# Recurrent stages of a two-layer hybrid block: where the high halves are cast, and one scan in place of two

## The chip, the cores and the metric

The kernel runs on one core of a Trainium2 chip. The metric is device time in microseconds (us) of one execution. A core has five engines with instruction queues of their own: TensorE (PE, matrix products, with its weight loads as PEld), VectorE (DVE), ScalarE (ACT), GpSimd (POOL) and SyncE (SP), which issues most of the transfers. Each engine works through its own queue in order; semaphores hold an instruction until what it needs is there.

## The reference, cut to what matters

Two layers are computed over 256 latent tokens and 256 context tokens of 1024 features. Each layer has a mixer (a gated linear recurrence beside a windowed attention, merged by learned gates) and a feed-forward part, both modulated by a condition. The part that concerns us is the recurrence: a centred convolution of width 4 over time, two gates from block-diagonal products (8 blocks of 128 channels), for each of two directions, and a linear scan. The forward scan runs through the context first and hands its last state to the latents; the backward scan does the same in reverse order.

```python
def _lru_coeffs(x, wa, ba, wx, bx, lam):
    r = jax.nn.sigmoid(_block_diag(x, wa, ba)).astype(jnp.float32)
    i = jax.nn.sigmoid(_block_diag(x, wx, bx))
    log_a = LRU_C * r * jax.nn.log_sigmoid(lam.astype(jnp.float32))
    a = jnp.exp(log_a)
    b = jnp.sqrt(-jnp.expm1(2.0 * log_a)) * (i * x).astype(jnp.float32)
    return a, b

def _rglru_branch(x_lat, x_ctx, conv_w, conv_b, wa, ba, wx, bx, lam, need_ctx):
    xl = _dwconv_centred(x_lat, conv_w, conv_b)
    xc = _dwconv_centred(x_ctx, conv_w, conv_b)
    ...
    hc_f = _linear_scan(ac_f, bc_f, None, False)
    hc_b = _linear_scan(ac_b, bc_b, None, True)
    ...
    hl = (_linear_scan(al_f, bl_f, hc_f[:, -1], False)
          + _linear_scan(al_b, bl_b, hc_b[:, 0], True))
    y_lat = hl.astype(x_lat.dtype)
    y_ctx = (hc_f + hc_b).astype(x_ctx.dtype) if need_ctx else None
    return y_lat, y_ctx
```

The second layer needs no output for the context, but its context recurrence still runs, since its last state starts the latents.

## The kernel before, in words

Activations lie with features on the 128 partitions and the 512 tokens along the free dimension, the 256 latents first and the 256 context tokens behind them. Every product of float32 values is made of three products: an operand is split into a high half, rounded to the type fp32r, and a low half, the rest. `mm3` (line 215 of the profile, through `mm`) issues high by high, high by low and low by high into one PSUM bank.

Weights arrive from memory in units of up to 1 MB (pool `wl`, 3 buffers). `split_half` turns 1024 columns of a unit into a high tile `wh` and a low tile `wlo` (4 buffers each): `hi_copy` makes the high half, on ScalarE (line 199) or on VectorE (line 201) by the next letter of `hi_pat`, and `lo_sub` makes the low half on VectorE (line 204). A new `wh` waits until TensorE has used the `wh` of four halves earlier.

The recurrent branch handles its 8 channel blocks in 4 groups of two. For a group, TensorE makes two projections `px` (48 products of 512 columns), two projections `pg` for the output gate (256 columns in the second layer), in the second layer one or more gated attention pieces, and then the gate products of two blocks (`gates`, 24 products, into the 4 PSUM buffers `pa`). Around them:

- `conv` takes `px` through ScalarE (line 876) and three VectorE steps (line 879) into `xf`, and splits it into a pair `xp` (casts of line 201, subtractions of line 204);
- `gates` drains each gate product with a sigmoid on ScalarE (line 893);
- `decays` makes tanh and exp on ScalarE (lines 902, 903) and multiplies the input gate with `xf` on GpSimd (line 904); a square root follows (line 937);
- `recur` makes, for each direction, two products (lines 910, 911) and the scan on VectorE: for the forward direction a scan of the context half (line 913) and one of the latent half that starts from its last column (line 915), for the backward direction one scan over all 512 columns in reverse (line 918). Sum, output gate and split follow (lines 921, 922, 201, and 204 on GpSimd).

The decays of a group are issued with the products of the next one, so that TensorE can go on. TensorE and SyncE keep the order in which the program is written. VectorE, ScalarE and GpSimd get theirs from a scheduler that weighs when inputs should be there; so the order on these engines can change around an edit. The stages in question run at about 252 to 400 us (first layer) and 980 to 1145 us (second layer).

Of the kernel before, what the change touches and what calls it, by code (L numbers as in the profile page):

```python
# [12 lines left out]
ALU = mybir.AluOpType  # L13
# [3 lines left out]
P = 128  # L17
D = 1024
KD = 8
S = 256  # L20
T = 512
L = 2
# [29 lines left out]

# Steps of the early products after the scores, the values and the turned probabilities
# of the last three iterations of the attention, per layer.
FILL = ((2, 0, 0, 2, 2, 0, 2, 0, 0), (2, 1, 0, 2, 1, 1, 1, 0, 0))

# Order of the first phase. A letter is a step, the number its piece:
# f, x, w: load modulation feature tile, token tile, weight unit
# M, C, A, B: modulation products, their row, the row turned to columns, scale and shift
# R, r, N: mean square, rstd, normalised token tile; T: transposed (feature tile, sample)  # L60
# h, H, L: modulated features, float32, high part, low part; K, V: key and value products
# u, U / s, S: high and low half of a weight unit / of a modulation tile
START = """
# [6 lines left out]
"""  # L70
START_F32 = (0, 1)  # modulation feature tiles multiplied as float32, without a split

# [67 lines left out]
def tile_hybrid_block(ctx: ExitStack, tc: tile.TileContext, xin, wstream, mod_start, mod_stream, c_rows,  # L140
# [54 lines left out]

# [1 line left out]
    def hi_copy(eng, dst, src):  # L197
# [23 lines left out]

# [1 line left out]
    dma_units = iter(UNITS)  # L223
# [73 lines left out]

# [1 line left out]
    vt = cst.tile([P, NVEC], F32, name="vt")  # L299
# [14 lines left out]

# [1 line left out]
    def mean_sq(src):  # L316
# [25 lines left out]

# [1 line left out]
    sc_ = cst.tile([P, 16], F32, name="silu_c")  # L344
# [15 lines left out]

# [1 line left out]
    mod_raw = {}  # L362
# [165 lines left out]

# [1 line left out]
    V.tensor_scalar(out=sk[:, 1, :], in0=sk[:, 0, :], scalar1=-1.0, scalar2=None, op0=ALU.mult)  # L530
# [6 lines left out]

# [1 line left out]
    lam = vt[:, VEC["lam", 0]:VEC["lam", 0] + 32]  # L539
# [26 lines left out]

# [1 line left out]
    gg = {}  # L568
# [22 lines left out]
    def mod_columns(l, ch, nv):  # L591
        """Shift or scale of a sublayer: a tile holds the weights of 128 features, one per partition."""
        which, is_sc = divmod(ch, 3)
        if not is_sc:
            for s in range(nv):
                c_bc[s] = tt([P, D])
                nc.sync.dma_start(out=c_bc[s], in_=c_rows[s].partition_broadcast(P))
                A.activation(out=c_bc[s], in_=c_bc[s], func=AF.Silu)  # L598
        cols = [sm.tile([P, KD], F32, tag="mcol", name=nm("mcol"), bufs=4) for _ in range(nv)]
        for ft in range(KD):  # L600
            raw = mod_next()
            for s in range(nv):
                junk = ut([P, D], BF16)
                V.scalar_tensor_tensor(out=junk, in0=raw, scalar=1.0, in1=c_bc[s], op0=ALU.mult, op1=ALU.mult,  # L604
                                       accum_out=cols[s][:, ft:ft + 1])
            if ft < KD - 1:
                yield
        for s in range(nv):
            dst = ab_of((l, which))[:, s, 1 - is_sc, :]
            V.tensor_tensor(out=dst, in0=cols[s], in1=vcol(("bmod", l), ch * 8, 8), op=ALU.add)  # L610
            if is_sc:
                V.scalar_tensor_tensor(out=dst, in0=dst, scalar=1.0, in1=vcol(("gfp" if which else "gmp", l), 0, 8),
                                       op0=ALU.add, op1=ALU.mult)
        if is_sc:
            c_bc.clear()
        yield
# [71 lines left out]
    for l in range(L):  # L688
# [4 lines left out]

# [1 line left out]
        def rope(ps, dst, ctx_too):  # L695
# [18 lines left out]

# [1 line left out]
        def scores(hd, q):  # L716
# [69 lines left out]

        # Products that don't wait for the attention fill its last iterations.
        pre_u, pre_p = [], []
# [51 lines left out]

# [1 line left out]
        tb = []  # L842
# [23 lines left out]

# [1 line left out]
        lead[0] = 100 * l  # L868
        yg = [None] * KD

        def conv(n, ps):
# [9 lines left out]
            xp = pair()  # L881
            split_sb(xf, xp[:, 0, :], xp[:, 1, :])
            return xf, xp

        def gates(n, i, u, xp):
            ri = []
            for dr in range(2):
                rt = tt([P, 2, T])
                for m, bk in ((0, "ba"), (1, "bx")):
                    ps = auxb()  # L890
                    wo = (i * 4 + dr * 2 + m) * P
                    mm3(ps, u.hi(wo, P), u.lo(wo, P), xp[:, 0, :], xp[:, 1, :], True, True)
                    A.activation(out=rt[:, m, :], in_=ps, func=AF.Sigmoid, bias=vcol((bk, l), dr * 8 + n))  # L893
                ri.append(rt)
            return ri

        def decays(n, ri, xf):
            ust = tt([P, 2, T])
            for dr in range(2):
                rt = ri[dr]  # L900
                li = l * 16 + dr * 8 + n
                A.activation(out=ust[:, dr, :], in_=rt[:, 0, :], func=AF.Tanh, scale=hsp[:, li:li + 1])
                A.activation(out=rt[:, 0, :], in_=rt[:, 0, :], func=AF.Exp, scale=nsp[:, li:li + 1])
                G.tensor_tensor(out=rt[:, 1, :], in0=rt[:, 1, :], in1=xf, op=ALU.mult)  # L904
            return ust

        def recur(n, ri, ust, gel):
            for dr in range(2):
                b, a, hs = ust[:, dr, :], ri[dr][:, 0, :], ri[dr][:, 1, :]
                V.scalar_tensor_tensor(out=b, in0=a, scalar=1.0, in1=b, op0=ALU.add, op1=ALU.mult)  # L910
                V.tensor_tensor(out=b, in0=b, in1=hs, op=ALU.mult)  # L911
                if dr == 0:
                    V.tensor_tensor_scan(out=hs[:, S:T], data0=a[:, S:T], data1=b[:, S:T], initial=0.0,  # L913
                                         op0=ALU.mult, op1=ALU.add)
                    V.tensor_tensor_scan(out=hs[:, 0:S], data0=a[:, 0:S], data1=b[:, 0:S],
                                         initial=hs[:, T - 1:T], op0=ALU.mult, op1=ALU.add)
                else:
                    V.tensor_tensor_scan(out=hs[:, ::-1], data0=a[:, ::-1], data1=b[:, ::-1], initial=0.0,  # L918
                                         op0=ALU.mult, op1=ALU.add)
            y = ri[0][:, 1, :N]  # L920
            V.tensor_tensor(out=y, in0=y, in1=ri[1][:, 1, :N], op=ALU.add)
            V.tensor_tensor(out=y, in0=y, in1=gel, op=ALU.mult)
# [3 lines left out]

        hi_pat[0] = "AV"

# [48 lines left out]

# [1 line left out]
        lead[0] = 50 * l  # L979
# [53 lines left out]

# [1 line left out]
        def row_mm(ps, u, kk, srcs, t, first, last):  # L1035
# [32 lines left out]
        class Chain:  # L1068
            """Norm of one token tile of the last product, residual and the next norm, in steps."""

# [211 lines left out]

# [1 line left out]
        def ff_gate(p1, p2):  # L1284
# [176 lines left out]
```

## Time and profile before

| | |
|---|---|
| three runs | 1380.54, 1381.34, 1384.61 us; median 1381.34 us |
| profiled execution, first to last instruction (span) | 1380.7 us; no other time of it is given, and what lies around the span is taken as 0.6 us, the median less the span |
| PE busy | 1329.4 us, 96% of the span |
| DVE busy | 1009.3 us, 73% |
| ACT busy | 649.5 us, 47% |
| POOL busy | 219.4 us, 16% |

The shares are means over the whole program. TensorE is busy nearly everywhere; where it is not, something else sets the pace, and that is read from windows and waits of that stretch. "Busy" of TensorE says that a product was under way, not at which clock; the granted clock stands beside it.

### The profile page before, as it was taken

Reading aid. Unit: us, or ns where it says so; the run is one execution under the profiler, and the core shown is the slowest. Engines: PE = TensorE matmul, PEld = TensorE weight load, DVE = VectorE, ACT = ScalarE, POOL = GpSimd, SP = SyncE. Lnnn points to the kernel's source line nnn. Section 1 sums busy time; section 2 is a strip of 40 time slices with the busy share of each in tenths; the row PEclk is TensorE's granted clock in tenths of the full one; section 3 lists DMA queues with packets and bytes.
Section 4 is the critical chain, followed back from the end, with each engine's and each line's share of the span. In section 5 each row is a group of like instructions: output and inputs, shape, how many; then the busy total and the mean of one; then the engine's idle time right before and its main releaser. Section 6 shows DMA issues by size and latency. Waiting matters only on the chain.

```text
span 1380.7 us, 18865 instructions
## 1 busy us (share of the span) xinstructions
PE 1329.4 (96%) x7372; PEld 1149.0 (83%) x7372; DVE 1009.3 (73%) x1497; ACT 649.5 (47%) x1026; POOL 219.4 (16%) x177
## 2 busy tenths in 40 slices
PE   6999999998989999999999999999999899899998
PEld 3978888876868889888888888899988688899897
DVE  6777687678998765948754754787879998655564
ACT  5766523386642354232212222577487555544342
POOL 1100010024420023101200120310013220102011
PEclk9999999999999999999999999999999999999999
DMA  8510464312257345374555442142333344355552
GB/s 326 211 64 32 138 229 153 106 54 99 92 165 261 123 151 215 107 273 169 191 192 211 162 159 92 62 154 92 108 107 122 122 153 183 123 185 182 193 178 87
DMA packets 37537, 207.98 MB, mean 151 GB/s; under 512 B 4292, under 2 KB 4420, under 8 KB 19784
## 3 DMA queue, kind: packets, MB, share of 16 engines
q1 hardware_dynamic: 37160, 206.24, 42.4%
q8 instruction: 58, 0.95, 0.3%
q10 hardware_dynamic: 288, 0.53, 0.1%
q14 instruction: 31, 0.25, 0.1%
HBM read 205.71 MB, written 1.05 MB: 150 GB/s over the span
## 4 chain that ended last, share of the span: by engine, by line
PE 74%; DVE 16%; issue 5%; ACT 3%; POOL 1%; DMA 0%; DVEq 0%; POOLq 0%; SPq 0%; ACTq 0%
PE pm L215 58%; PE pa L215 14%; DVE wlo L204 3%; DVE t L910 1%; DVE u L879 1%; DVE t L911 1%; DVE u L604 1%; PE pm L765 1%; ACT u L319 1%; DVE wh L201 1%; DVE t L204 1%; DVE t L918 1%; DVE t L913 1%; PE pa L341 1%; DVE t L201 1%
## 5 line engine op out<-in xcount | busy, mean ns | idle before, releaser
L215 PE MATMUL pm<-t,wh 128*128 128x512 f32 (+1 forms) x2672 | 705.4, 353 | 9.7 <-DVE wh L201 2.6
L215 PEld LDWEIGHTS pm<-t,wh 128*128 128x128 f32 x2672 | 473.6, 191 | 78.5 <-DVE wh L201 3.7
L215 PE MATMUL pm<-t,wlo 128*128 128x512 f32 (+1 forms) x1336 | 470.6, 352 | 12.0 <-DVE wlo L204 11.9
L204 DVE TENSOR_TENSOR wlo<-wl,wh 128x1024 fp32r<-128x1024 f32 x265 | 347.2, 1318 | 129.7 <-ACT wh L199 123.8
L199 ACT CAST wh<-wl 128x1024 fp32r<-128x1024 f32 x231 | 240.9, 1051 | 352.0 <-PE pm L215 270.1
L215 PEld LDWEIGHTS pm<-t,wlo 128*128 128x128 f32 x1336 | 255.5, 191 | 46.9 <-DVE wlo L204 14.0
L215 PE MATMUL pm<-wh,t 128*128 128x512 f32 (+1 forms) x784 | 229.0, 372 | 0.0
L215 PEld LDWEIGHTS pm<-wh,t 128*128 128x128 f32 x784 | 143.8, 188 | 25.5
L215 PE MATMUL pa<-t,wh 128*128 128x256 f32 (+1 forms) x768 | 157.2, 304 | 5.1 <-ACT t L893 2.8
L204 POOL TENSOR_TENSOR t<-u,t 128x256 fp32r<-128x256 f32 (+1 forms) x72 | 89.1, 1238 | 452.5 <-DVE t L201 334.5
L215 PE MATMUL pm<-wlo,t 128*128 128x512 f32 (+1 forms) x392 | 145.9, 372 | 0.1
L215 PEld LDWEIGHTS pa<-t,wh 128*128 128x128 f32 x768 | 123.7, 192 | 13.6 <-ACT t L893 8.1
L215 PE MATMUL pa<-t,wlo 128*128 128x256 f32 (+1 forms) x384 | 116.3, 303 | 0.0
L604 DVE SCALAR_TENSOR_TENSOR u<-t,t 128x1024 bf16<-128x1024 f32 x80 | 101.2, 1309 | 1.1 <-ACT t L598 1.1
L215 PEld LDWEIGHTS pm<-wlo,t 128*128 128x128 f32 x392 | 73.8, 188 | 13.2 <-DVE wlo L204 0.5
L215 PE MATMUL pa<-t,t 128*128 128x256 f32 (+1 forms) x480 | 78.0, 311 | 1.1 <-DVE t L204 1.1
L215 PEld LDWEIGHTS pa<-t,wlo 128*128 128x128 f32 x384 | 73.8, 192 | 2.7
L904 POOL TENSOR_TENSOR t<-t,u 128x512 f32<-128x512 f32 x32 | 52.4, 1661 | 101.6 <-ACT t L893 101.4
L215 PEld LDWEIGHTS pa<-t,t 128*128 128x128 f32 x480 | 64.7, 191 | 3.9 <-DVE t L204 1.7
L204 POOL TENSOR_TENSOR t<-t,t 128x512 fp32r<-128x512 f32 (+1 forms) x16 | 29.6, 1852 | 182.7 <-DVE t L201 137.8
L633 DVE SCALAR_TENSOR_TENSOR t<-t,silu_c,t 128x1024 f32<-128x1024 f32 x42 | 56.3, 1361 | 0.4
L329 POOL TENSOR_TENSOR c<-c,negh 128x1 f32<-128x1 f32 x26 | 16.5, 635 | 209.8 <-DVE c L327 193.6
(153 smaller groups left out, 1229.0 us busy)
## 6 DMA issues: line engine op xcount, KB each, us to landing
wl<-in_wstream SPq DMA_DIRECT2D x132, 1024.0 KB, 5.0
t<-in_mod_stream SPq DMA_DIRECT2D x80, 512.0 KB, 4.5
wl<-in_mod_start SPq DMA_DIRECT2D x6, 1024.0 KB, 5.2
wl<-in_wstream SPq DMA_DIRECT2D x12, 512.0 KB, 3.6
t<-in_xin SPq DMA_DIRECT2D x8, 512.0 KB, 4.7
t<-in_c_rows SPq DMA_DIRECT2D x5, 512.0 KB, 6.8
t<-in_mod_start SPq DMA_DIRECT2D x4, 512.0 KB, 8.3
t<-in_g_mix_post SPq DMA_DIRECT2D x3, 512.0 KB, 4.8
```

The source lines that it names most:

```text
L199: A.copy(dst, src)
L201: V.tensor_copy(dst, src)
L204: (G if eng == "G" else V).tensor_tensor(out=dst, in0=src, in1=hi.bitcast(F32), op=ALU.subtract)
L215: PE.matmul(o, lhsT=w, rhs=x, start=bool(start), stop=bool(stop))
L319: A.activation(out=junk[:, :src.shape[-1]], in_=src, func=AF.Square, scale=D ** -0.5, accum_out=ss)
L329: G.tensor_tensor(out=r, in0=ms, in1=negh, op=ALU.pow)
L341: PE.transpose(ps[:, i * P:(i + 1) * P], x[:, ft * P:(ft + 1) * P], ident)
L604: V.scalar_tensor_tensor(out=junk, in0=raw, scalar=1.0, in1=c_bc[s], op0=ALU.mult, op1=ALU.mult, accum_out=cols[s][:, ft:ft + 1])
L633: V.scalar_tensor_tensor(out=accs[s], in0=raw, scalar=cmod[s][:, k:k + 1], in1=accs[s], op0=ALU.mult, op1=ALU.add)
L765: PE.transpose(ps[:, k2, q2 * P:(q2 + 1) * P], probs[q0 + q2][:, (kt0 + k2) * P:(kt0 + k2 + 1) * P], ident)
L879: V.scalar_tensor_tensor(out=o, in0=pv[:, :, max(0, sh):S + min(0, sh)], scalar=cw[kk], in1=o, op0=ALU.mult, op1=ALU.add)
L904: G.tensor_tensor(out=rt[:, 1, :], in0=rt[:, 1, :], in1=xf, op=ALU.mult)
```

## The change

Four edits, all in the recurrent branch:

- `hi_pat` is "A" in place of "AV" during the branch: all high halves of weights there are cast on ScalarE, not every other one on VectorE. After the branch the pattern is as before.
- `conv` casts the high half of `xp` on ScalarE.
- The forward direction holds its values with the context ahead of the latents: its gate products read `xp` with the two halves swapped (a step backwards of 256 columns between the halves), and GpSimd reads `xf` in the same way.
- The forward scan becomes one instruction over 512 columns. The sum of both directions reads the forward result with its halves swapped and is written over the backward result.

The file also lost its comments, and lines behind 882 are numbered a few higher: 893 is now 901, 902 to 904 are 910, 911 and 915, 910 and 911 are 921 and 922, the scans are 925, 921 and 922 are 928 and 929, 937 is 944, 960 is 967.

```diff
             xp = pair()
-            split_sb(xf, xp[:, 0, :], xp[:, 1, :])
+            split_sb(xf, xp[:, 0, :], xp[:, 1, :], hi="A")
             return xf, xp
+
+        def swapped(v):
+
+            return v.rearrange("p (s t) -> p s t", s=2)[:, ::-1, :]
...
-                    mm3(ps, u.hi(wo, P), u.lo(wo, P), xp[:, 0, :], xp[:, 1, :], True, True)
+                    xh, xl = xp[:, 0, :], xp[:, 1, :]
+                    o = ps
+                    if dr == 0:
+                        o, xh, xl = ps.rearrange("p (s t) -> p s t", s=2), swapped(xh), swapped(xl)
+                    mm3(o, u.hi(wo, P), u.lo(wo, P), xh, xl, True, True)
...
-                G.tensor_tensor(out=rt[:, 1, :], in0=rt[:, 1, :], in1=xf, op=ALU.mult)
+                gx = rt[:, 1, :]
+                if dr == 0:
+                    gx = gx.rearrange("p (s t) -> p s t", s=2)
+                G.tensor_tensor(out=gx, in0=gx, in1=swapped(xf) if dr == 0 else xf, op=ALU.mult)
...
-                if dr == 0:
-                    V.tensor_tensor_scan(out=hs[:, S:T], data0=a[:, S:T], data1=b[:, S:T], initial=0.0,
-                                         op0=ALU.mult, op1=ALU.add)
-                    V.tensor_tensor_scan(out=hs[:, 0:S], data0=a[:, 0:S], data1=b[:, 0:S],
-                                         initial=hs[:, T - 1:T], op0=ALU.mult, op1=ALU.add)
-                else:
-                    V.tensor_tensor_scan(out=hs[:, ::-1], data0=a[:, ::-1], data1=b[:, ::-1], initial=0.0,
-                                         op0=ALU.mult, op1=ALU.add)
-            y = ri[0][:, 1, :N]
-            V.tensor_tensor(out=y, in0=y, in1=ri[1][:, 1, :N], op=ALU.add)
+                if dr == 1:
+                    a, b, hs = a[:, ::-1], b[:, ::-1], hs[:, ::-1]
+                V.tensor_tensor_scan(out=hs, data0=a, data1=b, initial=0.0, op0=ALU.mult, op1=ALU.add)
+            y = ri[1][:, 1, :N]
+            y2 = y.rearrange("p (s t) -> p s t", t=S)
+            V.tensor_tensor(out=y2, in0=swapped(ri[0][:, 1, :])[:, :N // S], in1=y2, op=ALU.add)
...
-        hi_pat[0] = "AV"
+        hi_pat[0] = "A"
```

The order on TensorE, SyncE and GpSimd stays the same, instruction for instruction. VectorE and ScalarE are scheduled anew in both recurrent stages. Two places of the first layer show it.

VectorE, at the end of the second group's recurrence, before: `wlo_3096` is the first low half that the third group's projections need; `t_` names are tiles of the recurrence (the scans are listed as SCALAR_TENSOR_TENSOR).

```order
L913 SCALAR_TENSOR_TENSOR t_2843<-t_2843,t_2932 128x256
L910 SCALAR_TENSOR_TENSOR t_2932<-t_2854,t_2932 128x512
L915 SCALAR_TENSOR_TENSOR t_2843<-t_2843,t_2932 128x256
L911 TENSOR_TENSOR t_2932<-t_2932,t_2854 128x512
L201 CAST wh_3095<-wl_2957 128x1024
L918 SCALAR_TENSOR_TENSOR t_2854<-t_2854,t_2932 128x512
L204 TENSOR_TENSOR wlo_3096<-wl_2957,wh_3095 128x1024
```

The same place on VectorE in the changed kernel, where the same low half is called `wlo_3092`:

```order
L925 SCALAR_TENSOR_TENSOR t_2841<-t_2841,t_2930 128x512
L929 TENSOR_TENSOR t_2830<-t_2830,u_2791 128x512
L921 SCALAR_TENSOR_TENSOR t_2930<-t_2852,t_2930 128x512
L201 CAST t_3031<-t_2830 128x512
L922 TENSOR_TENSOR t_2930<-t_2930,t_2852 128x512
L204 TENSOR_TENSOR wlo_3092<-wl_2955,wh_3091 128x1024
L925 SCALAR_TENSOR_TENSOR t_2852<-t_2852,t_2930 128x512
```

The cast of the high half has left VectorE, the two short scans are one, and the low half now stands ahead of the last scan of the group, not behind it.

ScalarE, in the first layer, from the convolution of the group's second block (`u_2779`) to its first sigmoid, before (`u_2791`, `u_2793` are the output gates, which wait for `pg`):

```order
L876 ACTIVATE u_2779<-pm_2670,vt 128x512
L199 CAST wh_2865<-wl_2727 128x1024
L960 ACT_TABLE_LOAD
L960 ACTIVATE u_2791<-pm_2729 128x512
L960 ACTIVATE u_2793<-pm_2754 128x512
L199 CAST wh_2947<-wl_2819 128x1024
L893 ACT_TABLE_LOAD
L893 ACTIVATE t_2821<-pa_2822,vt 128x512
```

The same stretch of ScalarE in the changed kernel:

```order
L876 ACTIVATE u_2779<-pm_2670,vt 128x512
L199 CAST wh_2787<-wl_2643 128x1024
L199 CAST wh_2863<-wl_2727 128x1024
L199 CAST wh_2867<-wl_2727 128x1024
L967 ACT_TABLE_LOAD
L967 ACTIVATE u_2791<-pm_2729 128x512
L199 CAST t_2784<-u_2779 128x512
L199 CAST wh_2945<-wl_2817 128x1024
L967 ACTIVATE u_2793<-pm_2754 128x512
L901 ACT_TABLE_LOAD
L901 ACTIVATE t_2819<-pa_2820,vt 128x512
```

Two more weight casts and the cast of the second block's `xp` (`t_2784`) stand between the convolution and the sigmoids, two of the casts now between the two output gates. No table load is added.

## Rows read from the trace of the kernel before

**Rows 1.** The page's first part: busy us, share of the span, instructions.

```profile
PE 1329.4 (96%) x7372; PEld 1149.0 (83%) x7372; DVE 1009.3 (73%) x1497; ACT 649.5 (47%) x1026; POOL 219.4 (16%) x177
```

**Rows 2.** Windows of both stretches: length, busy us (instructions) by engine, PEclk, DMA.

```profile
290.00:395.00 105.00, 93.57 (x399) 74.99 (x397) 101.35 (x131) 72.08 (x93) 39.09 (x19) 0.97 0.25 84
...
1017.00:1142.00 125.00, 114.44 (x744) 103.14 (x742) 122.70 (x159) 80.29 (x106) 29.52 (x19) 0.97 0.37 127
```

**Rows 3.** Waits of PE, 290:400, then 1000:1160: total us, times, longest.

```profile
PE pm L215 <- DVE wlo L204: 7.8, 2, 6.3
...
PE pm L215 <- DVE wlo L204: 4.1, 4, 1.2
```

**Rows 4.** Timeline of PE: start, us, line, operation, [idle before <-releaser].

```profile
337.34 0.80 PE L215 MATMUL pm<-t,wlo 128*128 128x512 f32 x1 [1.52 <-DVE wlo L204]
...
388.17 0.61 PE L215 MATMUL pm<-t,wh 128*128 128x512 f32 x2
395.05 0.79 PE L215 MATMUL pm<-t,wlo 128*128 128x512 f32 x1 [6.26 <-DVE wlo L204]
```

**Rows 5.** Timeline of DVE: casts and scans, each with what follows.

```profile
330.87 0.68 DVE L913 TENSOR_TENSOR_SCAN t<-t,t 128x256 f32<-128x256 f32 x1
331.47 1.72 DVE L910 SCALAR_TENSOR_TENSOR t<-t,t 128x512 f32<-128x512 f32 x1
333.12 0.74 DVE L915 TENSOR_TENSOR_SCAN t<-t,t 128x256 f32<-128x256 f32 x1
333.78 0.66 DVE L911 TENSOR_TENSOR t<-t,t 128x512 f32<-128x512 f32 x1
334.36 0.68 DVE L201 CAST wh<-wl 128x1024 fp32r<-128x1024 f32 x1
334.96 1.21 DVE L918 TENSOR_TENSOR_SCAN t<-t,t 128x512 f32<-128x512 f32 x1
336.10 1.19 DVE L204 TENSOR_TENSOR wlo<-wl,wh 128x1024 fp32r<-128x1024 f32 x1
...
356.45 0.40 DVE L201 CAST t<-u 128x512 fp32r<-128x512 f32 x1
356.77 0.68 DVE L910 SCALAR_TENSOR_TENSOR t<-t,t 128x512 f32<-128x512 f32 x1
```

**Rows 6.** Groups of DVE by form, 290:395: count, busy us, mean ns, idle before.

```profile
L204 DVE TENSOR_TENSOR wlo<-wl,wh 128x1024 fp32r<-128x1024 f32 x15 | 22.5, 1502 | 0.2
L910 DVE SCALAR_TENSOR_TENSOR t<-t,t 128x512 f32<-128x512 f32 x16 | 16.1, 1014 | 0.0
...
L201 DVE CAST wh<-wl 128x1024 fp32r<-128x1024 f32 x8 | 7.4, 926 | 0.0
...
L201 DVE CAST t<-u 128x512 fp32r<-128x512 f32 x6 | 2.5, 418 | 0.0
```

**Rows 7.** The same by form for 1017:1142.

```profile
L201 DVE CAST wh<-wl 128x1024 fp32r<-128x1024 f32 x13 | 10.5, 809 | 0.0
...
L201 DVE CAST t<-u 128x512 fp32r<-128x512 f32 x6 | 2.5, 420 | 0.1
```

**Rows 8.** Timeline where POOL and DVE run together.

```profile
302.18 5.01 POOL L204 TENSOR_TENSOR t<-t,t 128x512 fp32r<-128x512 f32 x1 [23.10 <-DVE t L201]
311.22 1.61 POOL L204 TENSOR_TENSOR t<-t,t 128x512 fp32r<-128x512 f32 x1 [4.03 <-DVE t L201]
...
306.02 2.25 DVE L204 TENSOR_TENSOR wlo<-wl,wh 128x1024 fp32r<-128x1024 f32 x1
```

**Rows 9.** ACT: casts, 290:395 by form; one whole line's min/median/max.

```profile
L199 ACT CAST wh<-wl 128x1024 fp32r<-128x1024 f32 x10 | 10.1, 1045 | 0.0
...
L1006 ACT ACTIVATE t<-u x16: 401/526/635, 426.3 to 1158.4; 128x512 fp32r<-128x512 f32 x8, 128x256 fp32r<-128x256 f32 x8
```

**Rows 10.** Waits of DVE's weight casts, 240:400, then 970:1180.

```profile
DVE wh L201 <- PE pm L215: 12.3, 2, 9.1
...
DVE wh L201 <- PE pm L215: 4.7, 4, 3.1
```

## The prediction

> **What bounds the kernel now.** I read the page's busy shares first. TensorE is at work for 96% of the span [rows 1], so the kernel as a whole can only gain where TensorE stands still or runs at a lower clock. The windows come next, laid over the two recurrent stages, since the edits touch nothing else. In 290 to 395 us TensorE is busy for 93.57 of 105 us and VectorE for 101.35; in 1017 to 1142 us TensorE for 114.44 of 125 and VectorE for 122.70 [rows 2]. There the reader is to see a change of roles: VectorE has 3.65 and 2.30 us of idle time left, and TensorE 11.43 and 10.56. ScalarE is busy for only 72.08 and 80.29 us. The waits then name the link: of what TensorE waits for, the low halves of weights on VectorE come first, 7.8 us in the first layer and 4.1 in the second [rows 3]. The timeline shows where: 1.52 us at 337.34, and 6.26 us before 395.05, where the products of the next projections have no low half [rows 4]. At 337.34 the instructions just ahead on VectorE are the cast, the backward scan and the subtraction itself, back to back [rows 5]. So in these two stretches the end is set by VectorE's queue, and what is taken out of it moves TensorE forward, as long as TensorE has idle time to give.
>
> The most that both stretches can return: the idle 11.43 + 10.56 = 22.0 us, and the clock. It was granted at 0.97 in both [rows 2]; with levels of 1.2 and 2.4 GHz, 3% of 105 and of 125 us is work lost, at most 3.2 and 3.8 us. Together 29.0 us.
>
> **Weight casts.** VectorE loses 24 casts of 128x1024 over the whole kernel. Eight stood in the first stretch and 13 in the second [rows 6, 7]; by the changed order two and four of them stay on VectorE, since they come when the branch has ended. So 6 and 9 go. The price of one is the distance to the next start, not the duration, because neighbours overlap: 334.96 - 334.36 = 0.60 us [rows 5]. That is 6 x 0.60 = 3.6 and 9 x 0.60 = 5.4 us. The means of 0.93 and 0.81 us [rows 6, 7] are longer, but hold the time that GpSimd costs (below), which the next instruction would meet instead.
>
> **Casts of the convolution.** Of 16, 6 lie in each stretch [rows 6, 7]; one costs 356.77 - 356.45 = 0.32 us [rows 5]. 6 x 0.32 = 1.9 us in each.
>
> **Scans.** A forward direction cost 0.60 us (331.47 - 330.87) and 0.66 (333.78 - 333.12) [rows 5]. A scan over 512 columns has a row of its own, the backward one: 336.10 - 334.96 = 1.14 us [rows 5]. 0.12 us less for each of 8 blocks is 1.0 us in each stretch. The forward one reads upward and not in reverse; I take the same price.
>
> **Order.** At the stall of 337.34 the low half now stands ahead of the group's last scan, not behind it: 1.1 us more there, once, by the same scan. In the second layer I count nothing for order.
>
> **What is added.** ScalarE takes over the casts: 6 x 1.045 us for weights and 6 x 0.635 for the convolution, 10.1 us on top of 72.08 in the first stretch, and 9 x 1.045 + 6 x 0.635 = 13.2 on top of 80.29 in the second [rows 2, 9]. The price for a 512-column cast from SBUF is the longest of line 1006. That gives 82 of 105 and 93.5 of 125 us, or 84% and 80% when each stretch is also shortened as forecast. It fits, so the casts themselves are hidden beside TensorE's products. If that cover were gone, they would cost up to those 23 us. The new waits are what remains: the subtraction for `xp` on VectorE now waits for a cast on another engine, with the next group's scans and low halves queued behind it. Bounds: nothing, if the other work put ahead of it in the new order covers the cast; 16 x 0.635 = 10.2 us if no cast is covered. A cast that comes earlier than on VectorE could even gain a little, but no row shows more than the cast's own 0.32 us, 5 us for 16. I take 1 us lost, near no cost, because in the listed order VectorE has several recurrence steps between the convolution and its subtraction.
>
> **Reversed halves.** 96 gate products (8 blocks, 2 gates, 3 products, 2 layers) and 16 multiplications on GpSimd read two runs of 256 columns in exchanged order. No row shows such a read on these engines. On VectorE the backward scan reads wholly in reverse at the price given. Lower bound: nothing, since the same number of columns is read, and fewer cannot be. Upper bound: every such read takes twice as long. Two products take 0.61 us [rows 4], so 0.3 us more for each, 96 x 0.3 = 29 us; on GpSimd 1.61 us more for each [rows 8], 16 x 1.61 = 26 us, beside other work. I take nothing, as the nearest row, the reversed scan, shows no price.
>
> **GpSimd's share.** In the first stretch the mean low half takes 1502 ns, the mean of line 910 is 1014 ns [rows 6]; undisturbed they take 1.19 and 0.68 us [rows 5]. That is 15 x 0.31 + 16 x 0.33 = 10 us of VectorE's time in two groups alone, spent where GpSimd runs: a GpSimd subtraction of 1.61 us took 5.01 us, and the low half on VectorE at 306.02 took 2.25 [rows 8]. It is tempting to hope that this goes with the casts. The Trainium skill (SBUF — State Buffer, "Who interferes with whom") says that an instruction of VectorE with two SBUF inputs contends with a GpSimd one just as a copy in a fast mode does, and that whichever starts first blocks the other. By that rule the stretching stays, since low halves, products and scans all have two inputs; the rows agree, as it is the low half and line 910 that are stretched. Were it the casts' doing, 10 us more would go. My sum leaves the 10 us where they are.
>
> **Sum.** First stretch 3.6 + 1.9 + 1.0 + 1.1 = 7.6 us, of 11.43 idle; second 5.4 + 1.9 + 1.0 = 8.3, of 10.56 idle. Together 15.9, less 1 for new waits: 14.9. Against the profiled execution: 1380.7 - 14.9 = 1365.8 us of span, and 0.6 around it: 1366.4, say 1366 us. The median shown is 1381.3. What is late next: still the low half after 388 us, with TensorE idle for a few microseconds there, so I count no gain of clock.
>
> **Rivals.**
> - *TensorE never waits in the stretches.* VectorE's queue gets so short that it is always ahead, and the clock stays up: 1381.3 - 29.0 = 1352 us. For it: the idle time of TensorE and what VectorE loses are of one size. Against it: GpSimd's share stays, and the last group's recurrence is a chain that depends on ScalarE's table loads as well. Chance 0.12, all that ends below 1357.
> - *ScalarE's queue eats the gain.* Each cast of the convolution comes late by its own length and the 16 waits cost their upper bound: 1381.3 - 15.9 + 10.2 = 1375.6, and 2 to 5 us more if weight halves come late too: 1378 to 1381. For it: ScalarE works in order, with table loads in between. Against it: a sixth of its time is free. Chance 0.11 for an end within the uncertainty.
> - *Slower: a weight cast blocks the sigmoids.* On VectorE the weight casts waited for TensorE to release a tile, 12.3 us in the first layer (9.1 us the longest) and 4.7 in the second [rows 10]. On ScalarE the output gates and sigmoids stand behind such a wait, and the sigmoids empty the four banks that TensorE fills. It decides from the point where one such wait is longer than TensorE needs to fill four banks, 12 products at 0.3 us or 3.7 us. If the gain is lost but for scans and convolution casts (5.8 us) and the 17 us are TensorE's: 1381.3 - 5.8 + 17.0 = 1392.5 us. Against it: the longest wait, 9.1 us, lay in front of a cast that the new order puts later. Chance 0.06.
> - *The exchanged halves cost at TensorE or GpSimd*: up to 1366 + 29 = 1395 us. The scan in reverse speaks against it. Chance 0.03.
>
> **How the numbers follow.** The likeliest case, VectorE's queue shortened and most of it returned, has 0.68 and reaches from 1357 to 1377 us. About 0.3% (4.1 us) is what a measurement of this kernel can tell from no change. Faster by more than that: 0.68 + 0.12 = 0.80. Within: 0.11. Slower: 0.06 + 0.03 = 0.09. The range for 8 in 10 is 1356 to 1379 us: the likeliest case, the edge of the first rival and the lower half of the second.
>
> **What would show it.** Right: in the changed profile VectorE's casts of weights fall by 24 and those from `u` by 16; the wait of 6.26 us near 395 shrinks by some 4 us or starts 7 to 8 us earlier; the group-to-group distance of the second layer's convolutions shrinks by about 2 us; gate products last as long as before. Wrong: VectorE idle for ScalarE's casts (its waits by `u` and `wh` over 5 us in a stretch), a wait of TensorE for sigmoids that takes the place of those for low halves, or longer gate products.

## The result, and the profile after

The changed kernel took 1366.51 us in the median of 4 runs (1366.32 to 1368.79), the kernel before 1382.7 us on the same chip (4 runs, 1380.54 to 1384.61). The ratio is 0.9887, with a 95% interval of 0.9871 to 0.9903. The prediction said 1366 us, in a range of 1356 to 1379. The profile of the changed kernel is that of its slowest run (1368.79 us, granted clock 0.990; the other three ran at 0.992 to 0.994), so it shows about 2.3 us less of the gain than the median.

The page's first part of the changed kernel, which answers to [rows 1] (span 1367.0 us):

```profile
PE 1323.8 (97%) x7372; PEld 1146.9 (84%) x7372; DVE 983.6 (72%) x1441; ACT 680.8 (50%) x1066; POOL 226.2 (17%) x177
```

VectorE has 56 instructions less (24 weight casts, 16 convolution casts, 16 scans) and ScalarE 40 more. The span is 13.7 us shorter. Of these TensorE's busy time gave 5.6 us (1329.4 to 1323.8) with the same 7372 products, and its idle time 8.1 us (span less busy: 51.3 to 43.2). I had expected nearly all of it from the idle time.

TensorE issues the same products in the same order in both kernels, so a stretch can be laid over exactly the same work. The windows of before, from a gate product of the first layer to the stall at 395.05, and from a gate product of the second layer to the first product behind its last group (length, then busy us and instructions of PE, PEld, DVE, ACT, POOL, then PEclk, DMA share, GB/s):

```profile
329.50:395.05 65.55, 55.09 (x230) 43.83 (x230) 62.17 (x78) 45.82 (x60) 25.83 (x13) 0.95 0.24 82
...
1062.30:1112.50 50.20, 43.75 (x252) 37.92 (x252) 49.85 (x65) 28.82 (x41) 14.07 (x10) 0.93 0.28 95
```

The same work in the changed kernel:

```profile
328.74:387.73 58.99, 52.87 (x232) 42.94 (x231) 55.20 (x64) 48.84 (x64) 27.13 (x13) 0.99 0.24 83
...
1059.10:1100.20 41.10, 39.99 (x253) 35.83 (x253) 40.72 (x50) 34.46 (x48) 19.04 (x10) 1.00 0.31 111
```

In the first pair 6.6 us go: 4.3 us of TensorE's idle time (10.46 to 6.12) and 2.2 of its busy time, at a clock of 0.99 in place of 0.95. In the second pair 9.1 us go: 5.3 us idle (6.45 to 1.11) and 3.8 busy, at 1.00 in place of 0.93. With the same products, the busy time changed almost only where the clock was lower in one of the two kernels, so I count it as clock. The windows of before that lie on the dips show it at the lower of the two levels (1.2 GHz):

```profile
1098.00:1105.00 7.00, 6.28 (x21) 4.94 (x20) 7.00 (x10) 3.81 (x6) 2.01 (x2) 0.52 0.44 152
337.00:340.50 3.50, 3.16 (x8) 2.49 (x9) 3.50 (x7) 3.00 (x5) 0.00 (x0) 0.51 0.20 26
```

Each of these two dips followed upon waits: 1.76 us for a high half at 335.10 and 1.52 for a low half at 337.34 [rows 4], and 1.54 and 0.64 us at 1096.30 and 1097.41. With these waits shortened neither dip is there after. The dip at the last stall of the first layer stayed, and costs more than before: 5.9 us of products ran in it (386.82 to 393.65), before 3.5 us (391.68 to 398.50), as the stall filled the rest. That gives 1.2 us back.

Waits of PE after, 290:400 and then 1000:1160, in the form of [rows 3]:

```profile
PE pm L215 <- DVE wlo L204: 5.4, 1, 5.4
...
PE pa L215 <- ACT t L901: 1.4, 2, 0.7
...
PE pm L215 <- DVE wlo L204: 3.0, 3, 1.2
...
PE pa L215 <- ACT t L901: 1.9, 4, 1.0
```

The 7.8 us of the first layer are 5.4, the 4.1 of the second 3.0; waits for sigmoids are 1.4 and 1.9 (1.8 and 1.0 before). The timeline of PE after, for the products that stand at 337.34 and 395.05 in [rows 4]:

```profile
332.85 0.39 PE L215 MATMUL pm<-t,wlo 128*128 128x512 f32 x1
...
387.73 0.80 PE L215 MATMUL pm<-t,wlo 128*128 128x512 f32 x1 [5.44 <-DVE wlo L204]
```

The wait at 337.34 is gone, and this product starts 4.5 us earlier. The stall of 6.26 us is still one of 5.44, but it begins 6.5 us earlier and ends 7.3 us earlier. The timeline of DVE shows why it still stands there:

```profile
383.72 1.22 DVE L925 TENSOR_TENSOR_SCAN t<-t,t 128x512 f32<-128x512 f32 x1
384.85 1.68 DVE L921 SCALAR_TENSOR_TENSOR t<-t,t 128x512 f32<-128x512 f32 x1
386.46 1.21 DVE L204 TENSOR_TENSOR wlo<-wl,wh 128x1024 fp32r<-128x1024 f32 x1
387.60 0.68 DVE L922 TENSOR_TENSOR t<-t,t 128x512 f32<-128x512 f32 x1
```

VectorE runs without a gap through the last group's recurrence and reaches the low half at 386.46; TensorE starts when it is done. Groups of DVE by form, 290:395, after (as in [rows 6]):

```profile
L204 DVE TENSOR_TENSOR wlo<-wl,wh 128x1024 fp32r<-128x1024 f32 x19 | 28.0, 1476 | 0.1
L925 DVE TENSOR_TENSOR_SCAN t<-t,t 128x512 f32<-128x512 f32 x16 | 19.3, 1209 | 0.0
L921 DVE SCALAR_TENSOR_TENSOR t<-t,t 128x512 f32<-128x512 f32 x14 | 13.1, 942 | 0.3 <-ACT t L944 0.3
```

In the same 105 us VectorE now makes 19 low halves, not 15. Their mean of 1476 ns and the 942 of line 921 (910 before) are nearly as stretched as before: what GpSimd costs (theory D below) has not gone with the casts.

### The profile page after: what moved, and what is told of

Same layout as the page of the kernel before. It is cut to its first block, busy times and chain, and to the rows that moved or that the text cites. A ratio compares the mean times of both kernels' runs of the same rounds, so it can differ in the third digit from the quotient of the medians.

```text
span 1367.0 us, 18844 instructions
## 1 busy us (share of the span) xinstructions
PE 1323.8 (97%) x7372; PEld 1146.9 (84%) x7372; DVE 983.6 (72%) x1441; ACT 680.8 (50%) x1066; POOL 226.2 (17%) x177
## 3 DMA queue, kind: packets, MB, share of 16 engines
HBM read 205.71 MB, written 1.05 MB: 151 GB/s over the span
## 4 chain that ended last, share of the span: by engine, by line
PE 77%; DVE 13%; ACT 4%; issue 4%; POOL 1%; DMA 1%; DVEq 0%; POOLq 0%; ACTq 0%
PE pm L215 61%; PE pa L215 14%; DVE wlo L204 3%; DVE t L925 2%; DVE u L604 1%; PE pm L765 1%; DVE t L921 1%; DVE t L922 1%; DVE t L204 1%; ACT u L319 1%; ACT wh L199 1%; DMA t<-in_xin 1%; DVE u L879 1%; PE pa L341 1%; DVE t L1108 1%
## 5 line engine op out<-in xcount | busy, mean ns | idle before, releaser
L199 ACT CAST wh<-wl 128x1024 fp32r<-128x1024 f32 x255 | 265.7, 1050 | 348.8 <-PE pm L215 270.7
L204 POOL TENSOR_TENSOR t<-t,t 128x512 fp32r<-128x512 f32 (+1 forms) x16 | 35.2, 2197 | 160.7 <-DVE t L201 140.1
```

Of the source, the lines that this page charges most:

```text
L199: A.copy(dst, src)
L204: (G if eng == "G" else V).tensor_tensor(out=dst, in0=src, in1=hi.bitcast(F32), op=ALU.subtract)
```

## The experiments

Theory A is that of the prediction: what leaves VectorE's queue in the two stages comes back on TensorE. Theory B says that it is the new order on VectorE and ScalarE, theory C that the high halves are ready earlier. Theory D says that what is left of the stretching is GpSimd's. Ratios are to the kernel before on the same chip, with their 95% intervals.

**Only the weight casts** (on the kernel before):

```diff
-        hi_pat[0] = "AV"
+        hi_pat[0] = "A"
```

> The kernel before with one edit: all high halves of weights in the recurrent branch are cast on ScalarE. Theory A (VectorE's queue time sets both stretches): 15 casts of 0.60 us leave the stretches, so 9.0 us less than before, 7 to 11. Theory B (the gain comes from the new order on VectorE, low halves ahead of scans): the gain can be anything up to the whole 14 us or near none, and the waits of TensorE change without VectorE's busy time mattering. Theory C (the cast on ScalarE runs beside VectorE, so the low half is ready earlier): the whole gain of the full change is here, 13 us or more.

Measured: 1374.44 us against 1381.8, ratio 0.9946 (0.9933 to 0.996), 7.4 us less. The first layer's stall ends only 1.4 us earlier (393.61), though six casts are gone there, and a new wait stands beside it. (This trace is 0.4 us late already at 249 us, ahead of anything edited.) Waits of PE of this kernel, 290:400:

```profile
PE pm L215 <- DVE wlo L204: 5.3, 1, 5.3
PE pa L215 <- ACT t L893: 4.5, 3, 3.1
```

TensorE waits 4.5 us for sigmoids (1.8 before), 3.14 us of it at 361.53. The timeline of ScalarE shows what these sigmoids, with their table load, stood for:

```profile
355.71 0.60 ACT L960 ACTIVATE u<-pm 128x512 f32<-128x512 f32 x1 [0.45 <-PE pm L215]
359.49 1.28 ACT L893 ACT_TABLE_LOAD   x1 [3.18 <-DVE t L918]
```

ScalarE had its casts behind it and stood idle until VectorE ended a backward scan (line 918, 358.17 to 359.39). So this is VectorE's queue once more, at another place, and not a weight cast that blocks the sigmoids, as the prediction's slower rival has it. In the full change TensorE's wait for sigmoids is 1.4 us.

**Only the convolution's cast** (on the kernel before):

```diff
-            split_sb(xf, xp[:, 0, :], xp[:, 1, :])
+            split_sb(xf, xp[:, 0, :], xp[:, 1, :], hi="A")
```

> The kernel before with one edit: the high half of the convolution's result is cast on ScalarE. Theory A: 12 casts of 0.32 us in the two stretches, 3.8 us less than before, 2 to 5. Theory B: no fixed size. Theory C: no gain or a small loss, since a hop to another engine is added in front of the gate products.

Measured: 1375.2 us, ratio 0.9954 (0.9942 to 0.9967), 6.4 us less. The 3.8 us of the casts lie outside the interval (4.6 to 8.0 us). The stall ends at 391.38, 3.7 us earlier. TensorE's idle time fell by just 3.8 us (span 1373.3 less busy 1325.8 is 47.5, against 51.3) and its busy time by 3.6: what is more than the casts' own time is busy time. Of that, 1.0 us lies ahead of 249 us and 0.6 behind 1151 us, where nothing was edited.

**Only the scan and the exchanged halves** (the changed kernel with both casts put back):

```diff
-        hi_pat[0] = "A"
+        hi_pat[0] = "AV"
...
-            split_sb(xf, xp[:, 0, :], xp[:, 1, :], hi="A")
+            split_sb(xf, xp[:, 0, :], xp[:, 1, :])
```

> The changed kernel with both casts put back as before: context ahead of latents and one forward scan are left. Theory A: 16 times 0.12 us, 2.0 us less than before, 1 to 4 with the order at the stall of the first layer. Exchanged halves read at a price (the rival of the prediction): up to 29 us more than before. Theory C: no change.

Measured: 1380.89 us, ratio 0.9986 (0.9977 to 0.9995), 1.9 us less by the ratio, with an interval of 0.7 to 3.2. With 96 gate products and 16 multiplications reading their halves exchanged, nothing of the 29 us that bounded them appears. The three parts alone sum to 0.54 + 0.46 + 0.14 = 1.14%, the whole change has 1.13%: within the intervals they neither help nor hinder each other.

**VectorE's time put back** (the changed kernel; copies of the casts' shapes into the low tiles, which the subtraction then overwrites; nothing waits for them; 24 of 128x1024 and 16 of 128x512; `rec` is 1 during the branch):

```diff
             hi_copy(hi_pat[0][hi_n[0] % len(hi_pat[0])], hi[:, :n], raw[:, s0:s0 + n])
+            if rec[0] and hi_n[0] % 2 == 1:
+                V.tensor_copy(lo[:, :n], raw[:, s0:s0 + n])
...
+            V.tensor_copy(xp[:, 1, :], xf)
             split_sb(xf, xp[:, 0, :], xp[:, 1, :], hi="A")
```

> The changed kernel, but VectorE makes a copy of the same shape and source for every cast that it lost (24 of 128x1024, 16 of 128x512), into the low half's tile ahead of the subtraction that overwrites it; nobody waits for the copies, and ScalarE makes the high halves as in the changed kernel. Theory A: only the scan is left of the gain, so 1 to 4 us less than before and 11 to 14 us more than the changed kernel. Theories B and C: the high halves still come from ScalarE, most of the gain stays, 10 us or more less than before.

Measured: 1382.04 us, ratio 1.0003 (0.9994 to 1.0012). The whole gain is gone, though ScalarE makes all the high halves and the scan is one. The timeline of PE of this kernel at the stall:

```profile
394.66 0.79 PE L215 MATMUL pm<-t,wlo 128*128 128x512 f32 x1 [5.62 <-DVE wlo L204]
```

It is back at the time of before (395.05). TensorE's busy time is back too, 1329.0 us. VectorE keeps the new order at the end of the second group's recurrence: the low half at 335.98, ahead of the scan at 337.11. So the gain, that of the clock with it, hangs on VectorE's time; B and C fall. Theory A had foretold 1 to 4 us less than before, for the one scan that stays; even that is not seen (0.8 less to 1.7 more by the interval).

**The gate product on VectorE** (the changed kernel):

```diff
-                G.tensor_tensor(out=gx, in0=gx, in1=swapped(xf) if dr == 0 else xf, op=ALU.mult)
+                V.tensor_tensor(out=gx, in0=gx, in1=swapped(xf) if dr == 0 else xf, op=ALU.mult)
```

> The changed kernel with the 32 multiplications of the input gate moved from GpSimd to VectorE. 28 of them lie in the two stretches and add 28 x 0.60 = 16.8 us to VectorE's queue. Theory D (what GpSimd runs beside VectorE is paid in VectorE's time, about 0.55 us for each GpSimd instruction: in 290 to 395 us of the changed kernel low halves, line 921, casts and line 604 are stretched by 11.0 us in all, beside 20 of them): 15.4 us come back, so within 4 us of the changed kernel. Rival (the stretching has another cause than GpSimd): 14 to 17 us more than the changed kernel, and the means of low halves and line 921 stay near 1476 and 942 ns.

Measured: 1361.23 us, ratio 0.9851 (0.9837 to 0.9864), some 5 us less than the changed kernel although VectorE got 32 instructions more. Theory D had foretold a difference of at most 4 us, its rival 14 to 17 us more; the gain goes beyond what D foretold.

**The low half of the result on VectorE** (the changed kernel):

```diff
-            split_sb(y, d[:, 0, :N], d[:, 1, :N], lo="G")
+            split_sb(y, d[:, 0, :N], d[:, 1, :N])
```

> The changed kernel with the 16 subtractions that split the recurrence's result moved from GpSimd to VectorE: 8 x 0.60 + 8 x 0.33 = 7.4 us more in VectorE's queue. Theory D: 16 x 0.55 = 8.8 us come back, so 0 to 3 us less than the changed kernel; the wait of ScalarE for GpSimd (3.75 us at 362 us) goes as well. Rival: 5 to 7 us more than the changed kernel.

Measured: 1370.64 us, ratio 0.9917 (0.9903 to 0.9931), some 4 us more than the changed kernel, where theory D foretold 0 to 3 less and its rival 5 to 7 more: a miss for both. The timeline of DVE of this kernel shows that the stretching goes on:

```profile
334.63 2.23 DVE L204 TENSOR_TENSOR wlo<-wl,wh 128x1024 fp32r<-128x1024 f32 x1
336.79 1.77 DVE L928 TENSOR_TENSOR t<-t,t 128x512 f32<-128x512 f32 x1
338.49 2.30 DVE L204 TENSOR_TENSOR wlo<-wl,wh 128x1024 fp32r<-128x1024 f32 x1
340.71 1.77 DVE L929 TENSOR_TENSOR t<-t,u 128x512 f32<-128x512 f32 x1
```

Low halves take 2.23 and 2.30 us, not 1.21, and lines 928 and 929 take 1.77, not 0.68. GpSimd's gate products, which remain, run beside them, four from 332.10 on for 9.82 us together, and TensorE waits 1.95 us at 336.92 for a stretched low half. Yet the time is not lost here: the stall at the end of this layer is 1.46 us and not 5.44, and behind it the same product starts at 393.06 us, in the changed kernel at 393.01. It is lost in the second layer. The timeline of PE of this kernel, and of the same product in the changed one:

```profile
1102.83 0.76 PE L215 MATMUL pm<-t,wh 128*128 128x256 f32 x2 [3.37 <-DVE wh L201]
```

```profile
1100.18 0.50 PE L215 MATMUL pm<-t,wh 128*128 128x256 f32 x2 [0.76 <-DVE wh L201]
```

At the last gate products the two kernels are level (1087.64 and 1087.60). Then TensorE waits 3.37 us for a high half that VectorE casts behind the last recurrence, and from there to 1109.70 the clock is granted at 0.51 (in the changed kernel at 1.00). In that recurrence lines 921 and 922 and the added subtraction took 1.77, 1.78 and 1.51 us, beside four gate products on GpSimd (8.04 us from 1088.30). That half a move shifted the meeting of both engines fits this, but is argued and not shown.

**No GpSimd in the recurrence** (both edits together):

> Both moves together: nothing of the recurrence runs on GpSimd. VectorE gets 24 us more work in the two stretches. Theory D: about 24 us come back, so within 5 us of the changed kernel, and the means on VectorE are those of undisturbed instructions (1.21 us a low half, 0.68 us line 921). Rival: 18 us or more above the changed kernel.

Measured: 1359.12 us (1358.46 to 1359.75), ratio 0.9833 (0.9819 to 0.9846): the fastest of all, 7.4 us below the changed kernel, where theory D had foretold a difference of at most 5. DVE by form, 290:395, of this kernel:

```profile
L204 DVE TENSOR_TENSOR wlo<-wl,wh 128x1024 fp32r<-128x1024 f32 x19 | 23.2, 1219 | 0.2
...
L921 DVE SCALAR_TENSOR_TENSOR t<-t,t 128x512 f32<-128x512 f32 x14 | 9.5, 687 | 1.0 <-ACT t L944 1.0
L915 DVE TENSOR_TENSOR t<-t,u 128x512 f32<-128x512 f32 x12 | 7.7, 689 | 0.0
```

Both means are at their undisturbed size, 1219 ns for 1476 and 687 for 942. On GpSimd a gate product took 1.71 us in the mean, here 0.69. TensorE's waits in 290:420 are nearly gone:

```profile
PE pa L215 <- ACT t L901: 1.4, 2, 0.7
PE pm L215 <- DVE wlo L204: 1.0, 2, 0.6
```

**More on ScalarE** (the changed kernel; the high half of the result `y` and the six weight casts left on VectorE):

```diff
-            split_sb(y, d[:, 0, :N], d[:, 1, :N], lo="G")
+            split_sb(y, d[:, 0, :N], d[:, 1, :N], hi="A", lo="G")
...
-        hi_pat[0] = "V"
+        hi_pat[0] = "A"
...
-                hi_pat[0] = "V" if j == 4 else "A"
+                hi_pat[0] = "A"
```

> The changed kernel with more of the same: the high half of the recurrence's result and the 6 weight casts that were left on VectorE go to ScalarE too. Theory A: 8 x 0.34 + 8 x 0.20 + 6 x 0.60 = 7.9 us leave VectorE's queue, but TensorE has only 6.8 us of waits left in 290 to 400 us and 6.8 in 1000 to 1160 us, so 4 to 7 us less than the changed kernel. Rival (ScalarE's queue, busy for 82 of 105 us, is the next bound): no gain, or up to 4 us more.

Measured: 1414.6 us, ratio 1.0234 (1.022 to 1.0248), 48 us more than the changed kernel. Both expectations missed. The two edits were then taken apart.

**The six weight casts alone:**

> The changed kernel with one edit: the high halves of the six weight casts of 128x1024 that stayed on VectorE behind each branch are cast on ScalarE too. Theory Q (what slowed the run with more on ScalarE was the cast of the recurrence's result, which holds ScalarE's queue until VectorE has finished the recurrence): six casts at 0.60 us leave VectorE where TensorE waits least, so 0 to 4 us less than the changed kernel, 1363 to 1367. Rival W (the six weight casts did it, by waiting for TensorE ahead of the sigmoids): over 1385, most of the 48 us.

Measured: 1366.77 us, ratio 0.9883 (0.9865 to 0.99): nothing against the changed kernel (1366.51).

**The cast of the result alone:**

> The changed kernel with one edit: the high half of the recurrence's result y is cast on ScalarE, 16 casts. Theory Q: nearly all of the 48 us that both edits cost together, 1405 to 1418, with ScalarE waiting over 40 us in total for the product with the output gate on VectorE (57 us with both edits). Rival W: within 6 us of the changed kernel, 1360 to 1372.

Measured: 1413.86 us, ratio 1.0228 (1.0212 to 1.0244): the whole 48 us. ScalarE's waits over the whole run, and then its timeline, of this kernel:

```profile
ACT t L199 <- DVE t L929: 61.8, 15, 8.4
```

```profile
308.56 0.62 ACT L199 CAST t<-t 128x512 fp32r<-128x512 f32 x1 [8.39 <-DVE t L929]
309.20 1.28 ACT L901 ACT_TABLE_LOAD   x1
310.49 3.12 ACT L901 ACTIVATE t<-pa,vt 128x512 f32<-128x512 f32 x5
```

The cast stands ahead of the sigmoids in ScalarE's queue and waits 8.39 us for the last product of the recurrence on VectorE (line 929). The sigmoids come late, the four banks stay full, and TensorE waits. Its timeline:

```profile
311.23 1.22 PE L215 MATMUL pa<-t,wh 128*128 128x512 f32 x2 [10.20 <-ACT t L901]
```

VectorE's busy time fell to 972.4 us here, 11 us below the changed kernel, and the kernel is 48 us slower.

**No GpSimd, and the six weight casts on ScalarE:**

> The version without GpSimd in the recurrence (gate product and low half of y on VectorE, 1359.1 us), and the six weight casts on ScalarE as well. Theory Q: VectorE is longer busy here, so the six casts are worth up to their 0.60 us each: 1355 to 1359. Rival W: over 1375. If the price of ScalarE's queue equals the gain: 1358 to 1361.

Measured: 1359.42 us, ratio 0.9833 (0.9818 to 0.9848), the same as without the six. Either these casts are not on the path, or ScalarE's queue costs what they are worth; the two are not told apart.

## Why the prediction was right, point by point

**What bounds the stages.** Right, and shown by the copies that gave the time back to VectorE: 1382.04 us. The sign foretold for the stall came nearly: it was to shrink by 4 us or start 7 to 8 us earlier, and it starts 6.5 and ends 7.3 us earlier, where the sum for the first stretch was 7.6.

**Term by term.** Since the products come in the same order, the traces tell where each kernel won its time. The same product starts at 249.28 us before and 248.32 after, ahead of anything edited; at the stall at 395.05 and 387.73; between the layers at 905.78 and 901.09; behind the second stretch at 1151.11 and 1138.47. The table has the lead won from the first to the second (first stretch) and from the third to the fourth (second), in us, from one trace of each kernel:

| Kernel | first, foretold | first, measured | second, foretold | second, measured |
|---|---|---|---|---|
| weight casts alone | 3.6 | 1.8 | 5.4 | 6.1 |
| convolution's cast alone | 1.9 | 2.7 | 1.9 | 1.6 |
| scan and exchanged halves alone | 1.0 | 2.3 | 1.0 | 0.7 |
| whole change (with 1.1 for order) | 7.6 | 6.4 | 8.3 | 8.0 |
| VectorE's time put back (the scan is left) | 1.0 | 1.0 | 1.0 | -0.8 |

Both sums are near what came, 15.9 foretold and 14.3 measured; single terms are off by a factor of about two. Of the 14.3 us, 8.5 are idle time of TensorE and the rest, near 5.9, its busy time. Between the stretches 1.2 us are lost behind the stall and 1.5 at a new dip (last section); 1.0 us ahead of 249 and 1.1 behind 1151 us are won where nothing was edited. That makes the 13.7.

**Luck.** The sum took 0.6 us for what lies around the span. In every run whose span is on record it is 1.8 us (1368.79 less 1367.0), and with that the forecast is 1367.6. That 1366 is met to half a microsecond is luck; that the gain is some 15 us is not.

**Weight casts.** 9.0 us predicted, 7.4 measured alone (5.5 to 9.3 by the interval). In the first layer the edit alone gave half of its 3.6 us, as TensorE came to wait for sigmoids that waited for VectorE; in the second it gave more than its 5.4.

**Casts of the convolution.** 3.8 predicted, 6.4 measured alone. The step that was mis-sized is the sentence on the clock: "I count no gain of clock." TensorE's idle time fell by the 3.8 us, the rest is its busy time, and 1.6 us of that lies where nothing was edited. In the full change, too, 14.9 us were to come from idle time, and 8.1 did; 5.6 came from busy time. The right total so rests on a split that was wrong. The dips at 337 and 1098 of before lasted 3.4 and 6.8 us; at half the clock they cost about half of that, 5.1 us together. That the stall after 388 us remains was foreseen, and its dip stayed; I took the one dip for all.

**Order.** The 1.1 us for the low half ahead of the scan have no run of their own. With the scan alone VectorE kept the old order there (the scan at 335.05, the low half at 336.19), and with VectorE's time put back the new order gained nothing over the whole kernel.

**Scans and exchanged halves.** 2.0 us predicted, 1.9 measured (0.7 to 3.2). That the numbers are so near is luck in part: of the 2.3 us in the first stretch 1.5 are busy time, for the dip at 337 is not there in this kernel either. The forward scan has the price of the reversed one, and the exchanged halves cost nothing that shows. The line of the scans over the whole program, the gate products by form, and the page's group of GpSimd's multiplication, after:

```profile
L925 DVE TENSOR_TENSOR_SCAN t<-t,t x32: 1193/1212/2205, 292.4 to 1127.0; 128x512 f32<-128x512 f32 x32
```

```profile
L215 PE MATMUL pa<-t,wh 128*128 128x512 f32 x128 | 40.6, 399 | 3.9 <-ACT t L901 3.9
...
L915 POOL TENSOR_TENSOR t<-t,u 128x512 f32<-128x512 f32 x32 | 53.9, 1710 | 103.0 <-ACT t L901 103.0
```

Before, the gate products' mean was 408 ns, and the median of GpSimd's multiplication 1734 ns (1735 after). Half of each group reads exchanged halves.

**What is added.** The prices of the casts on ScalarE were 1.045 and at most 0.635 us [rows 9]; they came out as 1.05 and 0.62 in the median:

```profile
L199 ACT CAST wh<-wl x255: 1029/1050/1080, 55.1 to 1339.2; 128x1024 fp32r<-128x1024 f32 x128
...
L199 ACT CAST t<-u x16: 606/620/632, 257.9 to 1084.9; 128x512 fp32r<-128x512 f32 x16
```

The new waits: the subtraction for `xp` waited for its cast for 1.5 us in 240:420, as little as assumed. A sign that I had named for wrong did show: VectorE waited 6.0 us for ScalarE's convolution step in 290:400 (3.5 before) and 14.2 us for high halves in 970:1160 (7.0 before, and 4.7 for tiles). It did not decide: TensorE's waits for low halves fell all the same, from 7.8 to 5.4 and from 4.1 to 3.0. A wait of the bounding engine counts only where something behind it is late.

**Where in the second layer.** "The group-to-group distance of the second layer's convolutions shrinks by about 2 us" was wrong. Line 876 there, before:

```profile
L876 ACT ACTIVATE u<-pm,vt x8: 758/762/779, 983.2 to 1080.2; 128x512 f32<-128x512 f32 x8
```

And after:

```profile
L876 ACT ACTIVATE u<-pm,vt x8: 759/762/776, 978.5 to 1078.5; 128x512 f32<-128x512 f32 x8
```

From first to last they take 100.0 us after and 97.0 before. The gain is not made a little in each group: the same product is 4.3 us earlier at 1005.8 of before, 3.2 at 1062.3, and 12.3 at 1112.5. It is made in the last group, by the shorter waits and the missing dip.

**GpSimd's share.** Left out of the sum, rightly: it stayed, and went when GpSimd's work went. The Trainium skill (SBUF — State Buffer, "Who interferes with whom") says that an instruction of VectorE with two SBUF inputs contends with a GpSimd instruction that reads SBUF, and the version without GpSimd agrees: 1219 ns where 1476 were, and 7.4 us less in all. GpSimd's order, said to be the same ahead of the prediction, differs in one place: a subtraction at 1045.6 us and the gate product at 1046.6 changed places (1041.6 and 1037.4 after). Nothing above hangs on it.

**The rivals.** That TensorE never waits (1352 us) fell with the 5.4 us stall that is left; without GpSimd the kernel comes nearer to it, 1359. That ScalarE's queue eats the gain fell in the full change. The slower rival's mechanism, a weight cast that waits for TensorE ahead of the sigmoids, is not behind the long waits. With the weight casts alone the waits for sigmoids grew by 2.7 us (1.8 to 4.5) in the first layer and 2.1 (1.0 to 3.1) in the second, but the longest in each (3.14 and 2.23 us) came from a scan on VectorE; with the whole change they are 1.4 and 1.9. With the cast of the result, which waits for VectorE ahead of the sigmoids, a wait of the same kind cost 48 us. The exchanged halves cost nothing.

Of the 5.6 us of busy time, 5.9 come from the two stretches, and 1.2 and 1.5 go back behind the stall and at the new dip; 1.3 ahead of 249 us and 1.1 behind 1151 us owe nothing to the edits. Open: how much of such gains another execution of the same kernels would show, since each has one trace.

## What to carry to other kernels

Ask of an instruction that you move to an engine with time to spare what it waits for, before what it lasts: 24 casts whose input lay ready gained 7.4 us, and the convolution's 16, whose input comes from VectorE soon after (ScalarE waited 8.0 us for it in all), gained 6.4. The 16 casts of the result, as short, waited 61.8 us for VectorE and cost 48 us, since all that stood behind them in the queue waited too. When the bounding engine shares something with a helper, compare the helper's price with its own: here 1.71 us on GpSimd, with VectorE stretched beside it, stood against 0.69 us on VectorE, and taking back all of the helper's work won where half of it lost. And when waits shrink, expect the clock to give back something as well, and leave room for it in the range: here 5.9 us of 14.3 in the two stretches, less 1.2 and 1.5 lost at two other dips.

## What was not expected of the hardware

The changed kernel has a dip of the clock that before has not, in a stretch where nothing was edited. Its window (columns as above):

```profile
881.00:886.00 5.00, 4.21 (x23) 4.02 (x24) 2.29 (x6) 4.04 (x8) 0.99 (x2) 0.66 0.01 3
```

The same product was 6.2 us earlier than before ahead of it and 4.7 behind. TensorE had been busy for 4.88 of the 7 us from 875 to 882. But it was so before, too, at the same products, and there the clock stayed at 1.00:

```profile
881.19:888.19 7.00, 4.88 (x40) 4.51 (x38) 5.29 (x12) 4.20 (x12) 2.78 (x4) 1.00 0.34 137
```

So a gain that was won at 395 us was in part given back 490 us later, with the same instructions on TensorE in the same order and the same share of work ahead of it. Of the other versions those with the scan alone, without GpSimd, with the six weight casts and with the result's cast on ScalarE have a dip at these products as well; those with one kind of cast alone, with VectorE's time put back, and with either of GpSimd's moves do not. What decides, the version or the single execution, is not shown.
